# The normed output of the state space heads transposed by DMA in 16-bit halves instead of on TensorE

## Chip, cores and metric

The kernel runs on one core of a Trainium2 chip. The metric is the time of one execution in device microseconds (us), as the median of some runs. The engines are called PE (TensorE, the matmuls), ACT (ScalarE), DVE (VectorE), POOL (GpSimd) and SP (SyncE, which here issues nearly all DMA transfers). Each runs its own row of instructions in order.

## What is computed

One layer of a decoder: 256 tokens, width 2048. The input projection feeds a state space part (4 groups) and an attention part; both meet in one output projection; a feed-forward layer and a per-layer embedding follow. What the change touches is the end of each state space group: y times SiLU(z), normed over the group's 512 columns, times the gain, into the output projection.

```python
proj = a_in @ w_in[i]                     # [z | x,B,C | dt | q | k | v]
xbc  = silu(causal_dwconv(xbc, conv_w, conv_b))
y = ssd(xs_h, dt, a_neg, B, C) + d_skip * xs_h
y = y.reshape(b, s, SSM_INNER) * silu(z)
y_ssm = rmsnorm(y.reshape(b, s, 4, 512), ssm_norm_g.reshape(4, 512))
h = h + concat([y_ssm, y_att]) @ w_out
```

## The kernel before

The 256 tokens are two blocks of 128 (b = 0 and 1). A product in float32 is made of three in the faster fp32r type: both factors are split into a high and a low part, and high x high (L219), high x low (L220) and low x high (L221) are summed in PSUM. In the first chunk, that of B and C, the three are L317 to L319.

Weights come in tiles "w" of 128 x 2 x 512 numbers (512 KB). SP loads each (L207) into a ring of eight buffers (WR, L31); ACT casts it to the high part wh (L192) and DVE subtracts for the low part wl (L193), each in a ring of four buffers (WB). One tile feeds 12 matmuls of 512 columns: two k, two blocks, three products. A chunk of the input projection is eight such tiles into one pair of accumulators (acc0, acc1, one for each block); two such pairs are in PSUM. PSUM also holds two tiles "tr" for transposes on PE and two small ones "ms".

The left factors must stand with the contracted dimension on the partitions, so activations are transposed. transpose_split (L245) does that on PE (L252, 128 x 128 each) and splits the result from PSUM: ACT writes the high part with the gain (L195), DVE the low part (L196). For one group of y that is 8 transposes and four splits.

The stages: the chunk of B and C with the loads of x and, at its end, the small matmuls for dt (L337, L338), a copy of their result (L341) and the evacuation L352; then for each group g of the state space part ssd_x (a chunk for x, L352, the convolution with transposes L279, evacuation L266 and L268 into the single buffer "xc", the scan up to L503), ssd_gate (a chunk for z, evacuated with SiLU by L511) and ssd_end (L515). ssd_end multiplies y by z (L518), takes the squares on ACT (L519), the root on POOL (L187), scales y (L522) and transposes and splits it into yh and yl. Group 0 is projected right behind the z chunk of group 1 (project, L373); groups 1 to 3 wait in a list and are projected during attention.

Attention begins with a chunk of queries (q0), one for k and one for v. norm_rope (L605) evacuates a block of q0 into "qkr", which has a single buffer (L607), squares it (L609), sums (DVE, L611), takes the root (L185, POOL L187), scales (DVE L613, POOL L614) and rotates it on POOL (L621 to L623); L633 transposes the result on PE. The feed-forward part already moves data with the method that the change brings to y: POOL takes the halves of 32-bit numbers apart (L775), SP issues a transposing DMA on 16-bit numbers (L777), POOL puts the halves together (L778).

The order of each engine's instructions is set when the kernel is built, by a scheduler with a modelled timeline and by the buffers of each pool; the code gives only dependencies and a first order. A change of a few instructions so moves others too.

Of the kernel before, what the change touches and what calls it, by code (L numbers as in the profile page):

```python
# [14 lines left out]
U16 = mybir.dt.uint16  # L15
# [5 lines left out]
P = 128  # L21
T = 256
# [5 lines left out]
KG = 4  # L28
KW = 2
WB = 4  # L30
WR = 8  # L31
LINE = 512

HD = 64
# [31 lines left out]
def hybrid_layer(  # L66
# [20 lines left out]
    nc = tc.nc  # L87
    V, S, G, PE = nc.vector, nc.scalar, nc.gpsimd, nc.tensor
# [13 lines left out]
    def nm(s):  # L102
        uid[0] += 1
        return f"{s}_{uid[0]}"
# [3 lines left out]
    def sb(pool, shape, tag, dt=F32, bufs=None):  # L108
        kw = {} if bufs is None else {"bufs": bufs}
        size = math.prod(shape[1:]) * (2 if dt in (mybir.dt.bfloat16, U16) else 4)  # L110
        tags = sizes.setdefault(pool.id, {})
        tags[tag] = max(tags.get(tag, 0), -(-size // 32) * 32 * (bufs or pool.bufs))
        return pool.tile(shape, dt, tag=tag, name=nm(tag), **kw)
# [10 lines left out]
    def tr_tile():  # L124
        return ps_tr.tile([P, NC], F32, tag="tr", name=nm("tr"))
# [14 lines left out]
    def load_first(k, pieces=1):  # L140

        xt = sb(xin, [P, T], "xt", bufs=6)
        nc.sync.dma_start(xt, xT[:, k, :])
        w = sb(wp, [P, KW, NC], "w", bufs=WR)
        n = KW // pieces
# [34 lines left out]
    g_attn, g_ffn, g_ple, g_ssm = (gn[:, i * KT : (i + 1) * KT] for i in range(4))  # L180
    posi = sb(const, [P, NB], "posi", I32)

    def rstd(ss, n, cols, tag):
        t = sb(small, [P, cols], "rs_t")
        V.tensor_scalar(t, ss, 1.0 / n, EPS, op0=ALU.mult, op1=ALU.add)  # L185
        r = sb(small, [P, cols], tag)
        G.tensor_tensor(out=r, in0=t, in1=nhalf[:, :cols], op=ALU.pow)  # L187
        return r

    def split(src, hi, lo, scale=None):  # L190
        if scale is None:
            S.copy(hi, src)  # L192
            V.tensor_tensor(out=lo, in0=src, in1=hi.bitcast(F32), op=ALU.subtract)  # L193
        else:
            S.activation(out=hi, in_=src, func=AF.Copy, scale=scale)  # L195
            V.scalar_tensor_tensor(out=lo, in0=src, scalar=scale, in1=hi.bitcast(F32), op0=ALU.mult, op1=ALU.subtract)  # L196

    def load_w(src, kt=KW, pieces=1):

        w = sb(wp, [P, KW, NC], "w", bufs=WR)  # L200
        wh = sb(wp, [P, KW, NC], "wh", F32R)
# [43 lines left out]
    def transpose_split(src, lhs, k0, gain=None):  # L245

        for half in range(2):
            tr = tr_tile().rearrange("p (a t) -> p a t", a=2)
            for i in range(2):
                f = half * 2 + i  # L250
                for b in range(NB):
                    PE.transpose(tr[:, i, b * P : (b + 1) * P], src[b][:, f * P : (f + 1) * P], ident)  # L252
            k = k0 + half * 2
            if gain is None:
                h, l = lhs.t[k // KG]
                j = k % KG
                split(tr, h[:, j : j + 2, :], l[:, j : j + 2, :])
            else:
                for i in range(2):
                    h, l = lhs.part(k + i)  # L260
                    split(tr[:, i, :], h, l, gain[:, k + i : k + i + 1])
# [36 lines left out]
    with xin_:  # L298
        wd = sb(xin, [P, KT, 32], "wd")
        dhl = sb(xin, [P, KT, 64], "dhl", F32R)  # L300
        for k in range(KT):
# [24 lines left out]
            if k in (5, 9):  # L326
                b = k // 4 - 1
# [20 lines left out]
    def evac_scaled(acc, pool, tag, bufs=None):  # L348
        res = []
        for b in range(NB):  # L350
            t = sb(pool, [P, NC], f"{tag}{b}", bufs=bufs)
            S.activation(out=t, in_=acc[b], func=AF.Copy, scale=rx[:, b : b + 1])  # L352
            res.append(t)
        return res
# [29 lines left out]
    with tc.tile_pool(name="ssd", bufs=1) as sp, tc.tile_pool(name="dram", bufs=1, space=bass.MemoryType.DRAM) as dp:  # L384
        BT = sb(sp, [P, 4, T], "BT")
        CT = sb(sp, [P, 4, T], "CT")
        for c, (acc, dst) in enumerate(((acc_b, BT), (acc_c, CT))):
            t = evac_scaled(acc, sp, "ct", 1)
# [117 lines left out]
        def ssd_gate(g):  # L506
            acc = in_chunk(3 + 2 * g)
            zs = []
            for b in range(NB):
                z = sb(sp, [P, NC], f"z{b}")  # L510
                S.activation(out=z, in_=acc[b], func=AF.Silu, scale=rx[:, b : b + 1])  # L511
                zs.append(z)
            return zs

        def ssd_end(g, y, zs):  # L515
            ssy = sb(sp, [P, NB], "ssy", bufs=2)
            for b in range(NB):
                V.tensor_tensor(out=y[b], in0=y[b], in1=zs[b], op=ALU.mult)  # L518
                S.activation(out=zs[b], in_=y[b], func=AF.Square, accum_out=ssy[:, b : b + 1])  # L519
            ry = rstd(ssy, NC, NB, "ry")  # L520
            for b in range(NB):
                V.tensor_scalar_mul(y[b], y[b], ry[:, b : b + 1])  # L522
            yT = Lhs(yp_, KG, "y")
            transpose_split(y, yT, 0, g_ssm[:, 4 * g : 4 * g + 4])
            return (yT, w_out, g, 1)

        y = ssd_x(0)
        zs = ssd_gate(0)

        with tc.tile_pool(name="rope", bufs=1) as rp:  # L530
# [3 lines left out]
            for j in range(HALF):  # L534
                f = float(np.float32(THETA) ** np.float32(-2.0 * j / ROPE))
# [51 lines left out]
        for g in range(4):  # L587
            held.append(ssd_end(g, y, zs))
            if g < 3:
                y = ssd_x(g + 1)  # L590
                zs = ssd_gate(g + 1)
            if g < 1:
                project(*held.pop(0))
# [5 lines left out]
    with tc.tile_pool(name="att_s", bufs=2) as as_, tc.tile_pool(name="att", bufs=2, reuse_waits="tile") as ap_, tc.tile_pool(name="ps_sc", bufs=1, space=PSUM) as ps_sc:  # L599
# [108 lines left out]
        for b in range(NB):  # L708
            n = norm_rope(acc, b, kg_, "k")
# [185 lines left out]
```

## Time and profile before

| | |
|---|---|
| median of 3 runs | 1459.9 us (1458.42 to 1459.93) |
| profiled execution | 1461.06 us, its span 1459.3 us |
| mean granted clock of PE | 0.999 of full speed |
| PE busy | 1449.4 us (99%), 6660 matmuls |
| DVE, ACT, POOL busy | 988.1 us (68%), 792.5 us (54%), 238.1 us (16%, 208 instructions) |
| chain that ended last | PE 95%, DVE 2% |

The span is the time from the first to the last instruction in the profile; the profiled execution has 1.8 us more around it. A timeline row gives the start, the duration, the engine, the source line, the operation, the tile written "<-" the tiles read, the shape and the count of instructions merged into the row, and in brackets the idle time ahead of it and what ended that. Matmuls are pipelined: the time from one start to the next is what one costs, not its duration. "SPq" is SP's own queue.

### The profile page before, as it was taken

The page shows a single profiled execution, that of the slowest core. Times are in us where ns is not written, and L with a number is a line of the kernel's source. Part 1 is how long each engine was busy: PE and PEld are TensorE (multiplying, and loading weights), DVE is VectorE, ACT ScalarE, POOL GpSimd, SP SyncE. Part 2 cuts the span into 40 slices and gives each one's busy share as a digit, 9 for nine tenths or more (in the row PEclk, how much of TensorE's full clock was granted, in tenths as well). Part 3 has the DMA queues.
Part 4 walks back from the last instruction along what each step waited for, and adds up shares of the span by engine and source line. Part 5 has one row for each costly group of instructions (what it writes and reads, how often), then busy time and mean ns, then how long its engine had stood idle before and what let it go on. Part 6 is the DMA issues. An engine that isn't in the chain of part 4 may idle for free.

```text
span 1459.3 us, 18328 instructions
## 1 busy us (share of the span) xinstructions
PE 1449.4 (99%) x6660; PEld 1178.8 (81%) x6660; DVE 988.1 (68%) x1272; ACT 792.5 (54%) x1103; POOL 238.1 (16%) x208
## 2 busy tenths in 40 slices
PE   9999999999999999999999999999999999999998
PEld 7787888888777777788888888888888888888887
DVE  6678876765859678665766756774675577476854
ACT  6575555645646455466565545544554564455653
POOL 0002010016033020003333201311320231020000
PEclk9999999999999999999999999999999999999999
DMA  9665656546554545568778668767886877776671
GB/s 330 227 192 201 199 179 187 159 159 171 162 167 148 162 135 168 158 185 219 212 209 232 210 192 225 215 202 205 209 220 193 213 209 217 201 212 188 212 222 56
DMA packets 125900, 283.19 MB, mean 194 GB/s; under 512 B 55473, under 2 KB 58353, under 8 KB 125425
## 3 DMA queue, kind: packets, MB, share of 16 engines
q1 hardware_dynamic: 125376, 281.55, 66.2%
q8 instruction: 52, 0.85, 0.2%
q10 hardware_dynamic: 432, 0.48, 0.1%
q14 instruction: 40, 0.32, 0.1%
HBM read 268.32 MB, written 2.13 MB: 185 GB/s over the span
## 4 chain that ended last, share of the span: by engine, by line
PE 95%; DVE 2%; POOL 1%; DMA 1%; ACT 1%; issue 0%; SPq 0%; DVEq 0%; POOLq 0%
PE acc L220 29%; PE acc L219 29%; PE acc L221 29%; PE acc L317 1%; PE acc L319 1%; PE acc L318 1%; PE sc L647 1%; PE ms L495 1%; PE tr L683 1%; PE tr L674 1%; PE tr L252 1%; DVE wl L193 1%; DMA seg<-scr 0%; POOL rs L187 0%; ACT wh L192 0%
## 5 line engine op out<-in xcount | busy, mean ns | idle before, releaser
L193 DVE TENSOR_TENSOR wl<-w,wh 128x1024 fp32r<-128x1024 f32 (+1 forms) x493 | 629.1, 1279 | 383.7 <-ACT wh L192 375.4
L192 ACT CAST wh<-w 128x1024 fp32r<-128x1024 f32 (+1 forms) x493 | 516.2, 1048 | 517.9 <-PE acc L221 452.1
L220 PE MATMUL acc<-wl,ah 128*128 128x512 f32 x1280 | 500.9, 391 | 1.4 <-DVE wl L193 1.4
L221 PE MATMUL acc<-wh,al 128*128 128x512 f32 x1280 | 499.5, 391 | 0.0
L219 PE MATMUL acc<-wh,ah 128*128 128x512 f32 x1280 | 498.6, 392 | 0.0
L220 PEld LDWEIGHTS acc<-wl,ah 128*128 128x128 f32 x1280 | 240.4, 188 | 53.1 <-issue 2.1
L219 PEld LDWEIGHTS acc<-wh,ah 128*128 128x128 f32 x1280 | 240.4, 188 | 51.5 <-issue 2.0
L221 PEld LDWEIGHTS acc<-wh,al 128*128 128x128 f32 x1280 | 240.4, 188 | 49.6 <-issue 0.5
L220 PE MATMUL acc<-wl,gh 128*128 128x512 f32 x352 | 137.0, 389 | 0.0
L221 PE MATMUL acc<-wh,gl 128*128 128x512 f32 x352 | 137.0, 389 | 0.0
L219 PE MATMUL acc<-wh,gh 128*128 128x512 f32 x352 | 136.4, 389 | 0.0
L775 POOL COPY half<-u 128x1024 uint16<-128x1024 uint16 x44 | 62.1, 1425 | 261.3 <-ACT u L773 261.2
L220 PE MATMUL acc<-wl,yh 128*128 128x512 f32 x256 | 101.5, 397 | 0.0
L219 PE MATMUL acc<-wh,yh 128*128 128x512 f32 x256 | 101.0, 396 | 0.0
L221 PE MATMUL acc<-wh,yl 128*128 128x512 f32 x256 | 100.8, 395 | 0.0
L778 POOL COPY uc<-flip 128x1024 uint16<-128x1024 uint16 x44 | 55.9, 1271 | 172.5 <-DMA flip<-half 172.5
L359 DVE TENSOR_TENSOR h<-h,acc 128x512 f32<-128x512 f32 x112 | 73.8, 679 | 5.8 <-PE acc L221 5.8
L220 PEld LDWEIGHTS acc<-wl,gh 128*128 128x128 f32 x352 | 66.1, 188 | 13.7
L219 PEld LDWEIGHTS acc<-wh,gh 128*128 128x128 f32 x352 | 66.1, 188 | 13.7
L221 PEld LDWEIGHTS acc<-wh,gl 128*128 128x128 f32 x352 | 66.1, 188 | 13.6
L268 DVE SCALAR_TENSOR_TENSOR cv<-uc,fcw,cv 128x254 f32<-128x254 f32 (+1 forms) x176 | 73.8, 479 | 0.0
L220 PEld LDWEIGHTS acc<-wl,yh 128*128 128x128 f32 x256 | 48.1, 188 | 12.2 <-issue 2.9
(229 smaller groups left out, 1123.6 us busy)
## 6 DMA issues: line engine op xcount, KB each, us to landing
w<-in_w_up_dram SPq DMA_DIRECT2D x176, 512.0 KB, 4.2
w<-in_w_in_dram SPq DMA_DIRECT2D x126, 512.0 KB, 3.9
w<-in_w_down_dram SPq DMA_DIRECT2D x88, 512.0 KB, 4.3
w<-in_w_out_dram SPq DMA_DIRECT2D x64, 512.0 KB, 3.7
w<-in_w_pg_dram SPq DMA_DIRECT2D x32, 512.0 KB, 4.2
seg<-scr SPq DMA_DIRECT2D x8, 512.0 KB, 5.2
xt<-in_xT_dram SPq DMA_DIRECT2D x16, 128.0 KB, 7.0
h<-in_x_dram SPq DMA_DIRECT2D x2, 1024.0 KB, 8.6
```

What stands on the lines that cost most here:

```text
L192: S.copy(hi, src)
L193: V.tensor_tensor(out=lo, in0=src, in1=hi.bitcast(F32), op=ALU.subtract)
L219: PE.matmul(acc[b], lhsT=hi, rhs=wh[:, i, :], start=(k == 0), stop=False)
L220: PE.matmul(acc[b], lhsT=hi, rhs=wl[:, i, :], start=False, stop=False)
L221: PE.matmul(acc[b], lhsT=lo, rhs=wh[:, i, :], start=False, stop=(k == total - 1))
L252: PE.transpose(tr[:, i, b * P : (b + 1) * P], src[b][:, f * P : (f + 1) * P], ident)
L268: V.scalar_tensor_tensor(out=dst[:, s:], in0=ps[:, : T - s], scalar=taps[n - 1 - s], in1=dst[:, s:], op0=ALU.mult, op1=ALU.add)
L317: PE.matmul(acc[b], lhsT=h, rhs=wh[:, c, :], start=(k == 0), stop=False)
L318: PE.matmul(acc[b], lhsT=h, rhs=wl[:, c, :], start=False, stop=False)
L359: V.tensor_tensor(out=hs, in0=hs, in1=acc[b], op=ALU.add)
L775: G.tensor_copy(half.rearrange("p (a n) -> p a n", a=2), u_.bitcast(U16).rearrange("p (n a) -> p a n", a=2))
L778: G.tensor_copy(uc[:, :, b * P : (b + 1) * P].bitcast(U16).rearrange("p f (t a) -> p f t a", a=2), flip.rearrange("p (a f) t -> p f t a", ...
```

## The change

In ssd_end the eight transposes of a group on PE go. For each block POOL copies the scaled y into two planes of 16-bit halves, in the buffer of z that is no longer needed; SP issues one transposing DMA into a tile "flip" of 16-bit numbers (two buffers); POOL copies the transposed halves together into a tile "yt" of 32-bit numbers. yt takes the single buffer "xc" of the convolution. The split into yh and yl then reads yt, four times 128 x 256. To make room the ring of w tiles has seven buffers instead of eight. For all four groups together that is 32 transposes on PE fewer, 16 copies on POOL and 8 transposing DMAs more. Lines behind the change have numbers higher by ten: L607 is L617, L633 is L643.

```diff
--- before.py
+++ after.py
@@ -28,7 +28,7 @@
 KG = 4
 KW = 2
 WB = 4
-WR = 8
+WR = 7
 LINE = 512
 
 HD = 64
@@ -518,10 +518,20 @@
                 V.tensor_tensor(out=y[b], in0=y[b], in1=zs[b], op=ALU.mult)
                 S.activation(out=zs[b], in_=y[b], func=AF.Square, accum_out=ssy[:, b : b + 1])
             ry = rstd(ssy, NC, NB, "ry")
+            yt = sb(sp, [P, 4, T], "xc")
             for b in range(NB):
                 V.tensor_scalar_mul(y[b], y[b], ry[:, b : b + 1])
+                half = zs[b].bitcast(U16).rearrange("p (a n) -> p a n", a=2)
+                G.tensor_copy(half, y[b].bitcast(U16).rearrange("p (n a) -> p a n", a=2))
+                flip = sb(sp, [P, 8, P], "flip", U16, 2)
+                nc.sync.dma_start_transpose(flip, half.rearrange("p a n -> p (a n)"))
+                G.tensor_copy(
+                    yt[:, :, b * P : (b + 1) * P].bitcast(U16).rearrange("p f (t a) -> p f t a", a=2),
+                    flip.rearrange("p (a f) t -> p f t a", a=2),
+                )
             yT = Lhs(yp_, KG, "y")
-            transpose_split(y, yT, 0, g_ssm[:, 4 * g : 4 * g + 4])
+            for f in range(4):
+                split(yt[:, f, :], *yT.part(f), g_ssm[:, 4 * g + f : 4 * g + f + 1])
             return (yT, w_out, g, 1)
 
         y = ssd_x(0)
```

The new order differs between the end of the B/C chunk and the first part of attention. In the names below the numbers count buffers. The first place is ACT around the SiLU evacuation of z of group 1 (L511), behind which project(0) starts. Before:

```order
L195 ACTIVATE yh0_215_1135<-tr_217_1137,gains_3_91 128x256
L195 ACTIVATE yh0_215_1135<-tr_218_1146,gains_3_91 128x256
L195 ACTIVATE yh0_215_1135<-tr_217_1137,gains_3_91 128x256
L195 ACTIVATE yh0_215_1135<-tr_218_1146,gains_3_91 128x256
L192 CAST wh_300_1561<-w_299_1560 128x1024
L192 CAST wh_303_1579<-w_302_1578 128x1024
L467 COPY Bt_224_1179<-tr_223_1177 128x128
L266 ACTIVATE xc_253_1331<-tr_254_1332,scw_15_133 128x256
L192 CAST wh_308_1601<-w_307_1600 128x1024
L511 ACT_TABLE_LOAD
L511 ACTIVATE z0_295_1554<-acc0_269_1408,rx_27_145 128x512
L511 ACTIVATE z1_296_1556<-acc1_270_1409,rx_27_145 128x512
```

and now:

```order
L192 CAST wh_294_1536<-w_293_1535 128x1024
L192 CAST wh_301_1560<-w_300_1559 128x1024
L192 CAST wh_304_1578<-w_303_1577 128x1024
L192 CAST wh_309_1600<-w_308_1599 128x1024
L511 ACT_TABLE_LOAD
L511 ACTIVATE z0_296_1553<-acc0_270_1407,rx_27_145 128x512
L511 ACTIVATE z1_297_1555<-acc1_271_1408,rx_27_145 128x512
L195 ACTIVATE yh0_218_1144<-xc_215_1133,gains_3_91 128x256 x4
L192 CAST wh_312_1618<-w_311_1617 128x1024
```

The four yh of group 0 stood nine instructions ahead of the table load and now stand right behind the second SiLU; they read xc, the tile yt, as one row "x4".

The second place is ACT at the entry to attention, with the evacuations of q0 (L607 before, L617 now) and the four yh of group 3; acc0_517, acc1_518 before and acc0_521, acc1_522 now are q0's accumulators. Before:

```order
L195 ACTIVATE yh0_502_2597<-tr_504_2599,gains_3_91 128x256
L195 ACTIVATE yh0_502_2597<-tr_505_2608,gains_3_91 128x256
L607 ACTIVATE qkr_543_2788<-acc0_517_2642,rx_27_145 128x512
L609 ACTIVATE qkn_544_2790<-qkr_543_2788 128x512
L195 ACTIVATE yh0_502_2597<-tr_504_2599,gains_3_91 128x256
L195 ACTIVATE yh0_502_2597<-tr_505_2608,gains_3_91 128x256
L192 CAST wh_583_2939<-w_582_2938 128x1024
L192 CAST wh_586_2957<-w_585_2956 128x1024
L607 ACTIVATE qkr_554_2817<-acc1_518_2643,rx_27_145 128x512
L192 CAST wh_589_2975<-w_588_2974 128x1024
L609 ACTIVATE qkn_555_2819<-qkr_554_2817 128x512
```

and now, where the casts to wh_623, wh_626, wh_629 and wh_632 are those of the first four tiles of the v chunk:

```order
L192 CAST wh_623_3064<-w_622_3063 128x1024
L192 CAST wh_626_3082<-w_625_3081 128x1024
L192 CAST wh_629_3100<-w_628_3099 128x1024
L195 ACTIVATE yh0_508_2603<-xc_505_2592,gains_3_91 128x256 x4
L192 CAST wh_632_3118<-w_631_3117 128x1024
L617 ACTIVATE qkr_547_2784<-acc0_521_2638,rx_27_145 128x512
L619 ACTIVATE qkn_548_2786<-qkr_547_2784 128x512
L617 ACTIVATE qkr_558_2813<-acc1_522_2639,rx_27_145 128x512
L619 ACTIVATE qkn_559_2815<-qkr_558_2813 128x512
L192 CAST wh_635_3136<-w_634_3135 128x1024
L192 CAST wh_638_3154<-w_637_3153 128x1024
L192 CAST wh_641_3172<-w_640_3171 128x1024
```

The two evacuations of q0 now stand next to each other, behind the cast of the fourth tile of v, and the later casts stand behind both.

The third place is PE where the v chunk starts (acc0_616, acc1_617 before, 620 and 621 now). Before:

```order
L220 MATMUL acc1_566_2847<-wl_590_2976,ah3_24_142 128x512
L221 MATMUL acc1_566_2847<-wh_589_2975,al3_25_143 128x512
L219 MATMUL acc0_616_3065<-wh_619_3068,ah0_18_136 128x512
L220 MATMUL acc0_616_3065<-wl_620_3069,ah0_18_136 128x512
L221 MATMUL acc0_616_3065<-wh_619_3068,al0_19_137 128x512
L219 MATMUL acc1_617_3066<-wh_619_3068,ah0_18_136 128x512
L220 MATMUL acc1_617_3066<-wl_620_3069,ah0_18_136 128x512
L221 MATMUL acc1_617_3066<-wh_619_3068,al0_19_137 128x512
L219 MATMUL acc0_616_3065<-wh_619_3068,ah0_18_136 128x512
```

and now, from the last matmul of the k chunk:

```order
L221 MATMUL acc1_570_2843<-wh_593_2971,al3_25_143 128x512
L219 MATMUL acc0_620_3061<-wh_623_3064,ah0_18_136 128x512
L220 MATMUL acc0_620_3061<-wl_624_3065,ah0_18_136 128x512
L221 MATMUL acc0_620_3061<-wh_623_3064,al0_19_137 128x512
L219 MATMUL acc0_620_3061<-wh_623_3064,ah0_18_136 128x512
L220 MATMUL acc0_620_3061<-wl_624_3065,ah0_18_136 128x512
L221 MATMUL acc0_620_3061<-wh_623_3064,al0_19_137 128x512
L219 MATMUL acc0_620_3061<-wh_626_3082,ah0_18_136 128x512
L220 MATMUL acc0_620_3061<-wl_627_3083,ah0_18_136 128x512
```

The next 16 matmuls write acc0_620 too, from the second, third and fourth tile, so that the first 24 of the chunk go to acc0; only then does acc1_621 come. Before, the two accumulators took turns from the start.

## Rows read from the trace of the kernel before

**Rows 1.** The page of the profile: busy time, share and count of PE, the subtraction on DVE (busy, mean ns of one, idle before), and the shares of the chain that ended last by engine.

```profile
PE 1449.4 (99%) x6660; PEld 1178.8 (81%) x6660; DVE 988.1 (68%) x1272; ACT 792.5 (54%) x1103; POOL 238.1 (16%) x208
...
PE 95%; DVE 2%; POOL 1%; DMA 1%; ACT 1%; issue 0%; SPq 0%; DVEq 0%; POOLq 0%
...
L193 DVE TENSOR_TENSOR wl<-w,wh 128x1024 fp32r<-128x1024 f32 (+1 forms) x493 | 629.1, 1279 | 383.7 <-ACT wh L192 375.4
```

**Rows 2.** The list of PE's waits over the whole span: what waited for what, us in total, times, longest.

```profile
PE acc L220 <- DVE wl L193: 1.4, 1, 1.4
PE tr L279 <- ACT ct L352: 1.2, 1, 1.2
```

**Rows 3.** PE's timeline around the eight transposes of y of group 0.

```profile
149.18 0.40 PE L221 MATMUL acc<-wh,al 128*128 128x512 f32 x1
149.42 1.04 PE L252 MATMUL tr<-ident,yc 128*128 128x128 f32 x8
150.21 0.48 PE L219 MATMUL acc<-wh,ah 128*128 128x512 f32 x1
150.53 0.39 PE L220 MATMUL acc<-wl,ah 128*128 128x512 f32 x1
150.76 0.40 PE L221 MATMUL acc<-wh,al 128*128 128x512 f32 x1
```

**Rows 4.** ACT's timeline at the end of the B/C chunk.

```profile
56.31 1.05 ACT L192 CAST wh<-w 128x1024 fp32r<-128x1024 f32 x1 [1.67 <-PE acc L319]
57.26 0.36 ACT L341 COPY hsq<-ms 64x256 f32<-64x256 f32 x1
57.52 1.25 ACT L352 ACTIVATE ct<-acc,rx 128x512 f32<-128x512 f32 x2
```

**Rows 5.** PE's timeline at the same place.

```profile
55.88 0.39 PE L319 MATMUL acc<-wh,al 128*128 128x512 f32 x1
56.11 0.28 PE L338 MATMUL ms<-ah,dhl 128*64 128x256 f32 x1
...
56.81 0.28 PE L338 MATMUL ms<-ah,dhl 128*64 128x256 f32 x1
58.31 0.41 PE L279 MATMUL tr<-ident,ct 128*128 128x128 f32 x2 [1.21 <-ACT ct L352]
```

**Rows 6.** PE's timeline at the transposition of the second block of q0.

```profile
341.13 0.39 PE L219 MATMUL acc<-wh,ah 128*128 128x512 f32 x1
341.94 0.66 PE L633 MATMUL tr<-ident,qkn 128*128 128x128 f32 x4 [0.42 <-POOL qkn L623]
```

**Rows 7.** ACT's timeline at the SiLU evacuation of z of group 1.

```profile
159.18 1.28 ACT L511 ACT_TABLE_LOAD   x1
160.47 1.27 ACT L511 ACTIVATE z<-acc,rx 128x512 f32<-128x512 f32 x2
161.63 1.05 ACT L192 CAST wh<-w 128x1024 fp32r<-128x1024 f32 x1
```

**Rows 8.** PE's timeline from the last matmul of that z chunk to the first of project(0).

```profile
160.22 0.39 PE L221 MATMUL acc<-wh,al 128*128 128x512 f32 x1
160.44 0.39 PE L219 MATMUL acc<-wh,yh 128*128 128x512 f32 x1
```

**Rows 9.** The tile "flip" of the feed-forward part: duration in ns (minimum, median, maximum), first and last start, and the time from a DMA's issue to its landing.

```profile
L777 SPq DMA_TRANSPOSE flip<-half x44: 1231/1233/2119, 662.4 to 1293.0; - x44
L778 POOL COPY uc<-flip x44: 1157/1162/2235, 667.0 to 1298.8; 128x1024 uint16<-128x1024 uint16 x44
...
DMA to landing us min/median/max: 3.9/5.6/7.1
```

**Rows 10.** The copy ahead of it, in the same form.

```profile
L775 POOL COPY half<-u x44: 1035/1041/2209, 658.5 to 1288.5; 128x1024 uint16<-128x1024 uint16 x44
```

**Rows 11.** ACT's timeline at the evacuation of q0 (L607 for block 0 and block 1).

```profile
318.22 1.05 ACT L192 CAST wh<-w 128x1024 fp32r<-128x1024 f32 x1 [1.67 <-PE acc L221]
319.17 0.83 ACT L195 ACTIVATE yh<-tr,gains 128x256 fp32r<-128x256 f32 x2
319.90 0.69 ACT L607 ACTIVATE qkr<-acc,rx 128x512 f32<-128x512 f32 x1
...
328.71 0.69 ACT L607 ACTIVATE qkr<-acc,rx 128x512 f32<-128x512 f32 x1 [3.13 <-POOL qkn L614]
```

**Rows 12.** ACT's timeline at a later evacuation of queries, again block 0 and block 1.

```profile
417.64 0.69 ACT L607 ACTIVATE qkr<-acc,rx 128x512 f32<-128x512 f32 x1 [0.39 <-PE acc L221]
...
423.84 0.69 ACT L607 ACTIVATE qkr<-acc,rx 128x512 f32<-128x512 f32 x1 [1.12 <-POOL qkn L614]
```

**Rows 13.** PE's timeline at its longest idle gap.

```profile
124.22 0.61 PE L219 MATMUL acc<-wh,ah 128*128 128x512 f32 x2
126.23 0.50 PE L220 MATMUL acc<-wl,ah 128*128 128x512 f32 x1 [1.40 <-DVE wl L193]
126.57 0.39 PE L221 MATMUL acc<-wh,al 128*128 128x512 f32 x1
```

**Rows 14.** PE's timeline at the start of the kernel.

```profile
11.16 1.88 PE L317 MATMUL acc<-wh,ah 128*128 128x512 f32 x4
12.86 0.41 PE L318 MATMUL acc<-wl,ah 128*128 128x512 f32 x1
13.11 0.39 PE L319 MATMUL acc<-wh,al 128*128 128x512 f32 x1
```

## Prediction, made before the changed kernel was run

> **What bounds the kernel now.** I read the page first, then the list of PE's waits, then single stretches of the timeline where the change touches something. The page [rows 1] shows PE busy 99% of the span and 95% of the chain that ended last, so any microsecond taken off PE's own work counts, and so does any microsecond for which PE has to wait. Other engines count only where PE comes to wait for them. The list of waits [rows 2] has 1.4 and 1.2 us as its longest: between PE's instructions there is next to nothing to win, and much room for a new wait to lose. The pace is that of a 512-column matmul, one each 0.23 us from start to start [rows 3], so a weight tile of 12 matmuls lasts 2.75 us and a chunk of eight tiles 22.0 us. PE, ACT, DVE, POOL and SP each run their own row of instructions in order; the question for every moved instruction is whether PE stands behind it.
>
> **What the change removes.** Each group's eight transposes of y run from 149.42 to 150.21, and the second matmul after them starts 0.32 after the first, not 0.23 [rows 3]: 0.79 + 0.09 = 0.88 us of PE, four times 3.52 us. No other engine hides that; all of it lies on the path. **-3.52.**
>
> Two effects of the new order go with it. At the end of the b/c chunk PE waits 1.21 us for ACT's evacuation [rows 5], which stands behind a cast that waits for the last L319 and behind L341, the copy of ms [rows 4]. In the new order ten, not seven, of the small L337/L338 matmuls stand behind that last L319. They start 0.115 us apart (56.11 to 56.81, six steps), so the cast can start 0.35 us earlier; but L341 still needs the last of them, which ends at 57.09, and L341 started at 57.26 already. The gain lies between 0.1 and 0.35, nearer the former since L341 is what is late next: **-0.15.** And the rotated queries of block 1 were transposed (L633) 0.81 us after the matmul before, where 0.23 is the pace [rows 6]; in the new order this transposition stands far behind its rotation: **-0.58.**
>
> **What it adds beside other work.** Sixteen POOL copies and eight transposing DMAs. The same three steps run 44 times in the FFN: the halves taken apart 1.04 us, the DMA 5.6 us to landing (7.1 at most), the halves put together 1.16 us (2.24 at most) [rows 9, 10]. POOL is busy for 16% of the span, so 16 copies, some 18 us, cost nothing as long as nobody waits for the 8 us that one chain takes. The split reads SBUF instead of PSUM: two PSUM tiles are left to the conv transposes. The ring of seven w tiles instead of eight covers 7 x 2.75 = 19 us against loads that land within some 4 to 5 us; SP loses 1.23 us per transposing DMA [rows 9]. I cost this at nothing; if a load were late it would show as a wait of ACT's cast for a w. The next group's conv must wait for the split's last read of the shared "xc" buffer; its first row in the order stands behind that split anyway, and the result is wanted a chunk later.
>
> **Where PE will wait (1): project(0).** In the order before, ACT makes the four yh well ahead of the Silu of z(1). In the new order they stand directly behind it (the first pair of order excerpts), and project(0)'s first matmul on PE stands directly behind z(1)'s last: PE, which passed here with no gap, 160.22 to 160.44 [rows 8], now waits for z0, z1 and the first yh. By ACT's times of before the table load ends and z0 starts at 160.47, the next instruction after z1 at 161.63 [rows 7]; a yh from SBUF takes about 0.5 us (two on tr take 0.83 together [rows 11]), so PE goes on at 162.15: 1.7 us lost. If ACT comes earlier, z1 is bound by PE alone: last matmul ends at 160.61, z1 lasts 0.69 and hands over after 0.59, yh 0.5, 0.06 to hand on: PE goes on at 161.8: 1.4 us. I take the middle: **+1.55.** The flips do not decide here: the second is issued at about 152, lands by 157.6 and is put together by 158.8, at worst 161.3 by the longest rows.
>
> **Where PE will wait (2): the entry to attention.** In the order before, ACT evacuated q0's first block (L607) among the casts of the k chunk, with nothing waiting for it [rows 11]. In the new order the four yh of group 3 stand between the third and fourth cast of the v chunk, and both evacuations of q0 (now L617) behind them (second pair of excerpts). The v chunk uses q0's accumulators, so PE stops at its first matmul until L617 has read acc0. The cast ahead of L617 needs the buffer of the k chunk's last tile, that is, PE at the end of k: 0.2 us later it starts (56.11 to 56.31, [rows 4, 5]), L617 follows 0.95 later (318.22 to 319.17, [rows 11]), lasts 0.69, and 0.1 goes for the handover: 1.95 us at least. Are the flips later than that? Counted from the start of the k chunk, SP issues the second flip of group 3 behind a load that needs the slot of k's last tile: four tiles of PE 11.0, wait and cast 1.25, the DVE subtraction 1.28 [rows 1], the load's issue 0.3: 13.8. Landing 5.6 and copy 1.16 make 20.6; the cast before the yh ends at about 20.5; four yh at 0.36 end at 22.0, and the fourth cast could not start before 22.2 anyway. So by the medians the flips cost nothing, by the longest rows (7.1 and 2.24) they end at 23.1 and the stall is 4.3. I take 2.4, near the medians. **+2.4.**
>
> Then PE has 24 matmuls of acc0 in a row (the third pair), 5.5 us, and needs acc1: L617 of block 1. It has one buffer "qkr", free when POOL's product of block 0 has read it: 6.2 us from one evacuation to the next where nothing is in the way (417.64 to 423.84 [rows 12]), 8.8 at this very place before (319.90 to 328.71 [rows 11]). I take 6.2, since ACT now waits in L617 with all later casts behind it and DVE therefore has no subtraction to run against POOL. PE begins 0.8 after L617 began, is through at 6.3, and may go on at 6.2 + 0.69 + 0.1 = 7.0: **+0.7**, or 3.3 by the longer row.
>
> **The sum.** -3.52 - 0.15 - 0.58 + 1.55 + 2.4 + 0.7 = **+0.4 us.** The profiled run took 1461.06 us, of which 1459.3 is the span; it would become 1461.5. The three timed runs have their median 1.2 us below it, 1459.9; I give the forecast on their footing: **1460.3 us**, no change that can be measured.
>
> **A rule of the Trainium skill that speaks against the change.** "VectorE: DVE Perf Modes", section "Rules for kernel authors", says to transpose 128x128 on TensorE if a PSUM destination will do, and by DMA otherwise. PSUM did do here. Its table of paths (section "The three transpose paths") counts 390 ns for one on TensorE; this trace has 0.11 us for one of eight in the pipeline [rows 3], and the trace decides. By the page's figure the estimate of the removed work would be 32 x 0.39 = 12.5 us, and the sum -8.6.
>
> **Rivals.** (A) The gain stands: no new wait, because ACT reaches the yh and q0 in time. Then -3.52 - 0.15 - 0.58 = -4.25, 1455.6 us. For it: PE's list of waits has hardly a row [rows 2], so the order has kept such things hidden before. Against it: in both places PE's next matmul reads what ACT has still to write. Chance 0.10, with the cases where one of the waits is missing and the other short.
>
> (B) Slower: the chain of q0's block 0 takes the 8.8 us of [rows 11], not 6.2. DVE's subtraction and POOL's power and product then run at the same time as before. The second stall is 3.3 instead of 0.7: 1462.9; with a flip that lands at 7.1 and a copy of 2.24 ahead of it the first is 4.3 instead of 2.4: 1464.8. It decides as soon as the second evacuation begins more than 8.7 us after the first. Chance 0.16.
>
> (C) The clock: at the start, before PE had run without gaps, 512-column matmuls stood 0.43 us apart until 12.86, then 0.25 [rows 14], the lower and the upper of the two levels, 1.2 and 2.4 GHz. After an idle gap of 1.40 at 124 to 126 us the next two stood 0.34 apart, the first of them 0.50 long, and the granted clock stayed up [rows 13]. The new gaps, 1.55 and 2.4, are little longer; if one of them brought the lower level for some 15 matmuls, it would cost 15 x 0.2 = 3 us: 1463.3. Chance 0.04. The Trainium skill, "TensorE: Matmul & The Clock Gate", section "Part 1: The HAM clock gate", says that the engine falls back to half its clock when it has been idle; by that rule (C) would follow, and the trace, where 1.4 us idle did not do it, agrees only that short gaps do no harm.
>
> **How the numbers follow.** About 0.2% (2.9 us) is what a measurement of this kernel can tell from no change: faster is under 1457.0, slower over 1462.8. The forecast has 0.70. Its ends: the first wait 1.4 to 1.7, the second 1.95 to 4.3 with most of it under 3, the third 0 to 2: 1459 to 1462.6; 1457.4 if one is cut short by an early ACT. Faster 0.10 is (A); slower 0.20 is (B) and (C). The range of 1457.4 to 1463.6 leaves out most of (A) and the double case of (B).
>
> **What the profile after would show.** No L252 with yc; POOL 224 instructions instead of 208, the new copies near 1.0 to 1.2 us; flips landing in 4 to 7 us. In PE's list of waits, acc waiting for yh of L195 near 160 us (about 1.5) and acc waiting for qkr of L617 near 335 to 343 us (about 2.4, then 0.7); the one for POOL's qkn gone. If the first two are absent, (A) is right; if the third is over 2.5, (B); matmuls 0.43 apart behind a gap would be (C). I would be wrong altogether if casts wait for w tiles, or if DVE's subtractions become slower wherever POOL copies run.

## The result and the profile after

The changed kernel takes 1461.49 us (median of 17 runs, 1460.27 to 1465.96), the kernel before in the same series 1459.43 us (median of 17). By the two medians it is 2.1 us slower. The ratio, which goes by all runs and not by the medians, is 1.0020 with a 95% interval of 1.0014 to 1.0027, that is 2.9 us (2.0 to 3.9). No change (1.0000) lies outside the interval, though the size is only about the 0.2% which the prediction took as the least that can be told. The profiled execution has a span of 1462.0 us, 2.7 more than that of before.

The page of the changed kernel answers to the first row of [rows 1]:

```profile
PE 1446.7 (99%) x6628; PEld 1176.0 (80%) x6628; DVE 988.8 (68%) x1272; ACT 793.2 (54%) x1103; POOL 264.8 (18%) x224
```

The 32 transposes are gone from PE (6660 to 6628), the 16 copies are on POOL (208 to 224). PE is 2.7 us less busy and the span 2.7 us longer, so PE stands idle longer than before. The list of PE's waits, to be held against [rows 2]: what waited for what, us in total, times, longest.

```profile
PE acc L219 <- ACT qkr L617: 2.3, 1, 2.3
PE acc L219 <- ACT yh L195: 2.2, 1, 2.2
...
PE tr L279 <- ACT ct L352: 1.1, 1, 1.1
PE tr L725 <- DVE s L721: 0.9, 1, 0.9
...
PE acc L220 <- DVE wl L193: 0.8, 1, 0.8
```

The first two rows are new and are the two places of the prediction: yh at project(0), qkr at the entry to attention. The fourth is new and was not foreseen: transposes of the second block of k. The wait for the rotated queries [rows 6] is gone, those at the B/C chunk and for wl are 0.1 and 0.6 shorter.

**Project(0).** PE's timeline, to be held against [rows 8]:

```profile
157.78 0.39 PE L221 MATMUL acc<-wh,al 128*128 128x512 f32 x1
160.41 0.50 PE L219 MATMUL acc<-wh,yh 128*128 128x512 f32 x1 [2.23 <-ACT yh L195]
160.75 0.39 PE L220 MATMUL acc<-wl,yh 128*128 128x512 f32 x1
...
161.54 0.63 PE L219 MATMUL acc<-wh,yh 128*128 128x512 f32 x1
161.96 0.63 PE L220 MATMUL acc<-wl,yh 128*128 128x512 f32 x1
```

From the last matmul of z(1) to the first of project(0) it takes 2.63 us instead of 0.22. And soon behind the gap the steps are 0.42 (161.54 to 161.96), not 0.23. ACT's timeline in the same stretch, against [rows 7]:

```profile
156.88 1.28 ACT L511 ACT_TABLE_LOAD   x1 [0.34 <-PE acc L221]
158.18 1.27 ACT L511 ACTIVATE z<-acc,rx 128x512 f32<-128x512 f32 x2
159.85 1.71 ACT L195 ACTIVATE yh<-xc,gains 128x256 fp32r<-128x256 f32 x4 [0.40 <-POOL xc L528]
```

The two z end at 159.45, and the yh begin 0.40 later, when POOL has put the second flip together. That copy, in POOL's timeline, and ahead of it the issue of its DMA in that of SP's queue:

```profile
152.79 1.24 SPq L527 DMA_TRANSPOSE flip<-z  x1
```

```profile
158.66 1.15 POOL L528 COPY xc<-flip 128x1024 uint16<-128x1024 uint16 x1 [2.56 <-DMA flip<-z]
```

**The entry to attention.** ACT's timeline, against [rows 11]:

```profile
333.82 1.05 ACT L192 CAST wh<-w 128x1024 fp32r<-128x1024 f32 x1 [1.67 <-PE acc L221]
335.55 1.71 ACT L195 ACTIVATE yh<-xc,gains 128x256 fp32r<-128x256 f32 x4 [0.68 <-POOL xc L528]
337.17 1.03 ACT L192 CAST wh<-w 128x1024 fp32r<-128x1024 f32 x1
338.10 0.68 ACT L617 ACTIVATE qkr<-acc,rx 128x512 f32<-128x512 f32 x1
...
344.33 0.69 ACT L617 ACTIVATE qkr<-acc,rx 128x512 f32<-128x512 f32 x1 [4.89 <-POOL qkn L624]
```

The chain is the one of the prediction, but with the flip 0.68 late, so that the yh and not PE's last matmul of k hold up the fourth cast (337.17). The second evacuation comes 6.2 us behind the first (338.10 to 344.33), as in [rows 12].

**The clock.** Windows of PE around both gaps: busy time of PE, PEld, DVE, ACT and POOL with counts, then the granted clock, the DMA share and GB/s.

```profile
157.20:160.40 3.20, 0.97 (x5) 0.47 (x3) 0.61 (x2) 2.79 (x5) 1.15 (x1) 1.00 1.06 366
160.40:164.90 4.50, 4.49 (x13) 3.54 (x14) 4.05 (x9) 3.00 (x6) 0.00 (x0) 0.62 0.39 148
165.00:170.00 5.00, 5.00 (x24) 4.12 (x23) 2.66 (x5) 1.97 (x3) 0.00 (x0) 1.00 0.25 89
338.80:342.40 3.60, 3.56 (x9) 2.86 (x10) 1.81 (x4) 0.63 (x1) 1.64 (x1) 0.53 0.59 199
```

The granted clock is 1.00 up to the gap, 0.62 in the 4.5 us behind the first and 0.53 in the 3.6 us behind the second: the lower level for most of these stretches, then 1.00 again. What it costs: 4.5 x 0.38 = 1.7 us and 3.6 x 0.47 = 1.7 us.

**The start.** The two profiles also differ where nothing was changed. Before, four L317 in a row began at 11.16 and took 1.88 us [rows 14]; the same four now:

```profile
9.57 1.20 PE L317 MATMUL acc<-wh,ah 128*128 128x512 f32 x4 [0.67 <-ACT wh L192]
```

PE came to the upper level earlier and stands 1.6 us ahead. That is an accident of this execution: in the second profile of the same program (experiment 5) the four begin at 10.54, behind steps of 0.43. So the difference of the two spans understates what the change costs in it.

**The sum of the two profiles.** Transposes -3.5; B/C -0.1; the wait for wl -0.6; L633 -0.6; project(0) 2.63 - 0.23 = +2.4, its slow steps +1.7; entry +2.5 (336.12 to 338.83 in PE's row, less 0.23), its slow steps +1.7; k's transposes +0.9; start -1.6. Together +2.8 of the measured 2.7; small moves elsewhere are left out.

The profiled execution took 1463.71 us, 2.2 more than the median. Where the clock stays up, PE waits another 0.6 at the second evacuation (experiment 5); without the slow steps and the start, the terms give -3.5 - 0.1 - 0.6 - 0.6 + 2.4 + 2.5 + 0.6 + 0.9 = +1.6. That is near the 2.1 of the medians, so most of the difference needs no slow steps. The 17 times fit this: nine lie from 1460.3 to 1461.5, six from 1462.1 to 1463.7 and two at 1465.9, where those of the kernel before lie from 1458.4 to 1461.4. That the upper ones are executions with slow steps is likely from the profiles, but not shown for each.

### The profile page after: what moved, and what is told of

It reads as the page before. It is cut to its first block, busy times and chain, and to the rows that moved or that the text cites. A ratio compares the mean times of both kernels' runs of the same rounds, so it can differ in the third digit from the quotient of the medians.

```text
span 1462.0 us, 18295 instructions
## 1 busy us (share of the span) xinstructions
PE 1446.7 (99%) x6628; PEld 1176.0 (80%) x6628; DVE 988.8 (68%) x1272; ACT 793.2 (54%) x1103; POOL 264.8 (18%) x224
## 4 chain that ended last, share of the span: by engine, by line
PE 92%; DVE 2%; DMA 2%; issue 1%; ACT 1%; POOL 1%; SPq 0%; DVEq 0%; POOLq 0%; ACTq 0%
PE acc L220 28%; PE acc L219 28%; PE acc L221 28%; PE tr L693 1%; PE sc L657 1%; DMA w<-in_w_in_dram 1%; PE ms L495 1%; DMA seg<-scr 1%; DVE wl L193 1%; PE tr L684 1%; PE acc L318 1%; PE acc L319 1%; PE acc L317 1%; PE tr L252 0%; ACT wh L192 0%
## 5 line engine op out<-in xcount | busy, mean ns | idle before, releaser
L788 POOL COPY uc<-flip 128x1024 uint16<-128x1024 uint16 x44 | 60.6, 1377 | 166.7 <-DMA flip<-half 166.6
L219 PEld LDWEIGHTS acc<-wh,yh 128*128 128x128 f32 x256 | 48.5, 189 | 13.3 <-ACT yh L195 2.7
```

What stands on the lines that cost most here:

```text
L219: PE.matmul(acc[b], lhsT=hi, rhs=wh[:, i, :], start=(k == 0), stop=False)
L788: G.tensor_copy(uc[:, :, b * P : (b + 1) * P].bitcast(U16).rearrange("p f (t a) -> p f t a", a=2), flip.rearrange("p (a f) t -> p f t a", ...
```

## Experiments

Ratios are to the kernel before, measured on the same chip in the same series, with 95% intervals; they go by all runs and so differ a little from the ratio of the two medians.

| kernel | median us | before | ratio (interval) |
|---|---|---|---|
| ring of 7, y on PE | 1459.24 | 1459.56 | 0.9988 (0.9967 to 1.0010) |
| only group 0 by DMA | 1462.47 | 1459.56 | 1.0026 (1.0016 to 1.0036) |
| groups 1 to 3 | 1462.32 | 1459.56 | 1.0021 (1.0012 to 1.0030) |
| groups 1 and 2 | 1458.22 | 1459.56 | 0.9992 (0.9984 to 1.0001) |
| the change again | 1462.11 | 1459.19 | 1.0021 (1.0012 to 1.0030) |
| the change, first gap filled | 1461.88 | 1459.19 | 1.0019 (1.0010 to 1.0027) |
| own pool, project(0) later | 1457.78 | 1459.19 | 0.9992 (0.9983 to 1.0001) |
| groups 0 to 2, project(0) later | 1457.50 | 1459.19 | 0.9985 (0.9977 to 0.9994) |
| own pool | 1462.14 | 1459.69 | 1.0015 (1.0007 to 1.0024) |
| project(0) later | 1460.95 | 1459.69 | 1.0009 (1.0000 to 1.0018) |
| groups 0 to 2, project(0) later, two qkr | 1455.09 | 1459.69 | 0.9970 (0.9959 to 0.9982) |
| all four, own pool, project(0) later, two qkr | 1460.39 | 1459.69 | 1.0004 (0.9995 to 1.0013) |

### 1. The shorter ring alone

```diff
-WR = 8
+WR = 7
```

> The kernel before with seven w buffers instead of eight, y still transposed on PE. Theory (the time of the changed kernel is made of two waits of PE, at project(0) and at the entry to attention): no difference to the kernel before, within 1 us, and no cast waits for a w. Rival (the shorter ring costs time by itself): about 2 us slower, with waits of casts for w in the profile.

No difference can be seen, and no cast waits for a w behind the first chunk. The rival's 2 us lie outside the interval. The ring is not where the time went.

### 2 to 4. Some groups only

```diff
+            if g in (0,):          # (1, 2, 3) and (1, 2) in the other two
                 yt = sb(sp, [P, 4, T], "xc")
...
+            else:
+                transpose_split(y, yT, 0, g_ssm[:, 4 * g : 4 * g + 4])
```

> Only group 0 is transposed by DMA, groups 1 to 3 on PE as before; seven w buffers. Theory: the 0.9 us of its transposes are gone, PE waits at project(0) for yh as in the changed kernel (2.2 us), and if the clock falls behind that gap, another 1.7 us: 1.5 to 3.2 us slower than before, and no wait for qkr at the entry to attention. Rival (each group's copies and transposing DMAs cost about the same, spread over the run): a quarter of the change's 2 us, 0.5 us slower, without one long wait.

> Groups 1 to 3 by DMA, group 0 on PE as before. Theory: -2.6 us of transposes, no wait for yh at project(0), the wait for qkr at the entry to attention as in the changed kernel (2.3 us) and up to 1.7 us of low clock behind it: between 0.5 faster and 2 slower than before. Rival (cost spread evenly over groups): 1.5 us slower with no long wait.

> Groups 1 and 2 by DMA, groups 0 and 3 on PE as before. Theory: both places keep their old order, neither wait appears, and 1.8 us of transposes are saved: 1.5 to 2 us faster than before. Rival (cost spread evenly over groups): 1 us slower.

One group of four, the first, costs 2.9 us by itself; the two in the middle are 1.3 faster, a little short of what was expected and with an interval that just touches no change. Groups 1 to 3 missed their expectation: 2.8 slower, not 2 at most. So the cost is not spread over groups; it comes with the first and the last. It can't be added up from the parts, though: 2.9 and 2.8 make 5.7, and all four together cost 2.1, since each kernel has its own order and so its own waits. The waits of PE, first with group 0 alone:

```profile
PE tr L731 <- DVE s L727: 2.2, 1, 2.2
PE acc L219 <- ACT yh L195: 1.9, 1, 1.9
```

with groups 1 to 3:

```profile
PE acc L219 <- ACT qkr L623: 3.7, 1, 3.7
```

and with groups 1 and 2:

```profile
PE tr L731 <- DVE s L727: 1.6, 1, 1.6
```

(L623, L727 and L731 are L617, L721 and L725 of the changed kernel.) yh is waited for with group 0 and qkr with group 3, each where expected. The wait for the transposes of k's second block also stands in kernels whose entry to attention is untouched: that was in no theory, and it is part of what group 0 alone costs and of what groups 1 and 2 do not save. With group 0 alone the terms are +2.0 at project(0), +2.2 for k, -0.9 for the transposes and -0.6 for L633, together +2.7: the larger half lies at k. Why k's block comes late there stays open; experiment 11 shows only what removes it.

### 5. The changed kernel once more

> The changed kernel once more. Theory (two waits of 2.2 to 2.4 us and, in some executions, 1.7 us of low clock behind each): 1 to 4 us slower than before, the waits for yh and for qkr again in the list; the steps of 0.43 us behind them may come behind one wait and not behind the other. Rival (the clock behind the gaps falls every time): both stretches of 0.43 us again.

The first gap again has slow steps behind it, the second has not. PE's timeline at both:

```profile
161.74 0.79 PE L219 MATMUL acc<-wh,yh 128*128 128x512 f32 x1 [2.63 <-ACT yh L195]
162.33 0.63 PE L220 MATMUL acc<-wl,yh 128*128 128x512 f32 x1
162.75 0.63 PE L219 MATMUL acc<-wh,yh 128*128 128x512 f32 x1
...
339.89 0.50 PE L219 MATMUL acc<-wh,ah 128*128 128x512 f32 x1 [2.21 <-ACT qkr L617]
340.24 0.40 PE L220 MATMUL acc<-wl,ah 128*128 128x512 f32 x1
340.48 0.40 PE L221 MATMUL acc<-wh,al 128*128 128x512 f32 x1
...
346.14 0.50 PE L219 MATMUL acc<-wh,ah 128*128 128x512 f32 x1 [0.47 <-ACT qkr L617]
```

Here the steps behind the second gap are 0.24, and so PE is through its 24 matmuls of acc0 before the second evacuation is done and waits once more, 0.86 us from start to start (345.28 to 346.14 in PE's row): the third wait of the prediction, which the slow clock had covered in the first profile. The clock behind the gap so differs between two executions of one program, so the rival, the same slow steps every time, is out.

### 6. The first gap filled

```diff
+                for _ in range(busy):          # 10, ahead of project(0)'s first product
+                    PE.matmul(acc[0], lhsT=aT(0, 0)[0], rhs=w[0][:, 0, :], start=True, stop=True)
```

> The changed kernel with ten matmuls more on PE between the last of z(1) and the first of project(0): they write project(0)'s accumulator ahead of its start and are overwritten, and they lie within the 2.6 us in which PE waited for yh. Theory: the wait's end is ACT's and does not move, the idle time shrinks to some 0.3 us, and behind it the steps are 0.23 us in every profile: up to 1.7 us faster than the changed kernel. Rival (the slow steps come from operands that have just been written, or the added matmuls delay the work): still 0.43 behind, the same time or up to 2.3 us more.

PE's timeline (L229 is the added line):

```profile
157.09 0.39 PE L221 MATMUL acc<-wh,al 128*128 128x512 f32 x1
157.31 2.43 PE L229 MATMUL acc<-wh,ah 128*128 128x512 f32 x10
159.59 0.39 PE L219 MATMUL acc<-wh,yh 128*128 128x512 f32 x1
159.81 0.39 PE L220 MATMUL acc<-wl,yh 128*128 128x512 f32 x1
160.04 0.40 PE L219 MATMUL acc<-wh,yh 128*128 128x512 f32 x1
```

The first product with yh starts 2.5 us behind the last of z(1), about as late as before, and the steps behind it are 0.22 from the first on. Operands just written do not slow PE: it reads a yh just written at 0.22 to 0.23 a step here, and also with group 0 alone, behind a gap of 1.87. That the filling kept the clock up is likely but not shown by one profile, since the clock stayed up behind some unfilled gaps too. The median, 0.2 us below the changed kernel's in the same series, doesn't show the 1.7: the clock does not fall behind every gap, and the gap at the entry to attention is still there. So the price of the clock is shown in profiles, not in medians.

### 7 and 8. Two ways around both waits

```diff
-WR = 7
+WR = 6
...
+    yx = mix.enter_context(tc.tile_pool(name="yx", bufs=1))
...
-            yt = sb(sp, [P, 4, T], "xc")
+            yt = sb(yx, [P, 4, T], "yt")
...
-                flip = sb(sp, [P, 8, P], "flip", U16, 2)
+                flip = sb(yx, [P, 8, P], "flip", U16, 2)
...
                 y = ssd_x(g + 1)
+                if g == 1:
+                    project(*held.pop(0))
                 zs = ssd_gate(g + 1)
-            if g < 1:
-                project(*held.pop(0))
```

The second kernel has only the last part of this, with seven w buffers, and keeps group 3 on PE (experiments 2 to 4 show how).

> The changed kernel with yt and flip in a pool of their own, which outlives that of the state space part, so that the buffers of attention come free as soon as the last transposing DMA has read, and with project(0) behind the x chunk of group 2 instead of directly behind the z chunk of group 1; six w buffers for room. Theory: neither wait appears, 3.5 us of transposes stay saved: 2.5 to 4 us faster than before. Rival (the costs lie in the copies, the DMAs or the shorter ring): about as slow as the changed kernel.

> Groups 0 to 2 by DMA, group 3 on PE, project(0) behind the x chunk of group 2; seven w buffers. Theory: neither wait appears and 2.6 us of transposes are saved: 2 to 3 us faster than before, less what the transposes of k's second block wait. Rival (cost with each group transposed by DMA): 1 to 2 us slower.

Both are on the fast side of before, by 1.4 and 1.7 us; for the first the interval just touches no change, and its expectation of 2.5 to 4 was missed. The second, expected 2 to 3 faster less the wait of k's block (1.6 in its list), did a little better than that. Neither has a wait for yh or qkr in its list. Its longest row in the first, and in the second:

```profile
PE tr L644 <- POOL qkn L634: 1.8, 2, 1.6
```

```profile
PE tr L731 <- DVE s L727: 1.6, 1, 1.6
```

With the two long waits gone, the next chain in line shows: the norm and rotation of q and k on POOL.

### 9 and 10. Each way alone

The diffs are the two parts of the one above, the first with six w buffers.

> The changed kernel with yt and flip in a pool of their own that outlives the state space part's; six w buffers for room; project(0) where it was. Theory (q0's evacuation waited for the memory that yt and flip held): the wait for qkr at the entry to attention is gone, the wait for yh at project(0) of 2.2 to 2.6 us stays: 1 to 2.5 us faster than the changed kernel, within 1 us of the kernel before. Rival (the evacuation stands late for another reason): the wait for qkr stays, no faster than the changed kernel.

> The changed kernel with project(0) behind the x chunk of group 2 and nothing else; seven w buffers. Theory: the wait for yh at project(0) is gone, the one for qkr of 2.2 us and more stays: 2 to 3 us faster than the changed kernel, within 1 us of the kernel before. Rival (the wait only moves to the next place that needs yh): a wait for yh elsewhere, same time as the changed kernel.

With the own pool, ACT's timeline at the entry to attention (L618 is L617 of the changed kernel, L196 is L195):

```profile
317.77 0.68 ACT L618 ACTIVATE qkr<-acc,rx 128x512 f32<-128x512 f32 x1
...
321.02 1.71 ACT L196 ACTIVATE yh<-yt,gains 128x256 fp32r<-128x256 f32 x4 [0.43 <-POOL yt L529]
```

The evacuation stands ahead of the yh, twenty microseconds earlier than the 338.10 of the changed kernel, and nothing waits for it: what held it was the memory of yt and flip, which attention's buffers take over (the ring went to six w buffers with it, which was not varied alone). But the time was not won: 1462.14 is 2.4 us slower than before, where at most 1 was expected. The list of waits:

```profile
PE tr L644 <- POOL qkn L634: 1.9, 2, 1.6
PE acc L220 <- ACT yh L196: 1.4, 1, 1.4
...
PE tr L478 <- ACT xc L473: 0.9, 1, 0.9
```

The wait for yh became shorter because PE meets another one ahead of it (xc, 0.9), and the rotated queries are waited for instead of qkr. The theory was right on the cause and wrong on the worth.

With project(0) later alone the wait for yh is gone and appears nowhere else, but the one at the entry grew:

```profile
PE acc L219 <- ACT qkr L617: 3.8, 1, 3.8
```

The stretch of slow steps behind it was longer too (13 matmuls at 0.43 or near it). The kernel is 1.3 us slower than before, a little over the microsecond that was expected at most, and gains less on the changed kernel than the expected 2 to 3 (ratio 1.0009, there 1.0020).

### 11 and 12. A second buffer for qkr

```diff
-            r = sb(ap_, [P, NC], "qkr", bufs=1)
+            r = sb(ap_, [P, NC], "qkr", bufs=2)
```

added to the kernels of 8 and of 7.

> Groups 0 to 2 by DMA, group 3 on PE, project(0) behind the x chunk of group 2, seven w buffers, and qkr with two buffers instead of one. Theory (with one qkr buffer the second block of k is normed a chain later, and its transposes make PE wait 1.6 us): that wait shrinks, 1 to 1.6 us faster than the same without the second buffer, 3 to 4 us faster than before. Rival (POOL's chain sets the time, not the buffer): the wait stays, no difference.

> All four groups by DMA, yt and flip in a pool of their own, project(0) behind the x chunk of group 2, qkr with two buffers, six w buffers. Theory: neither of the two long waits, 3.5 us of transposes saved, and the wait for rotated queries (1.8 us with one qkr buffer) shorter or later: 2 to 4 us faster than before. Rival (six w buffers or PE waiting for the rotation eat it): within 1 us of the kernel before, with waits for qkn or for w in the list.

The first is the fastest kernel of the study: 4.6 us below before, ratio 0.9970. Its whole list of waits, from the longest:

```profile
PE acc L317 <- ACT wh L192: 1.5, 2, 1.0
PE tr L279 <- ACT ct L352: 1.1, 1, 1.1
PE ms L155 <- PEq L901: 0.8, 1, 0.8
PE acc L220 <- DVE wl L193: 0.8, 1, 0.8
```

Behind the first 125 us there is no wait left, the one for k's second block included. It gained more than that wait's 1.6. Neither the second qkr buffer nor the later project(0) was tried on the kernel before with y on PE, so how much of the 4.6 us is owed to the transposing DMAs stays open. The other kernel missed its expectation: 0.7 us slower than before, not 2 to 4 faster. Its longest wait:

```profile
PE tr L644 <- POOL qkn L634: 3.1, 2, 2.8
```

and PE's timeline there:

```profile
333.24 0.66 PE L644 MATMUL tr<-ident,qkn 128*128 128x128 f32 x4 [2.84 <-POOL qkn L634]
...
333.96 0.39 PE L221 MATMUL acc<-wl,ah 128*128 128x512 f32 x1
334.19 0.39 PE L222 MATMUL acc<-wh,al 128*128 128x512 f32 x1
```

With two buffers the product of block 1 stands on POOL between the rotations of block 0, and PE's transposes of block 0 are in its row already. So with all four groups by DMA the entry to attention remains the weak place, whichever way it was arranged here.

## Why the prediction was right, and where its terms were not

The forecast was 1460.3 us and no measurable change; 1461.5 came out, in the range, and the direction that it gave for the sum, a little slower, was the one measured. But the slowdown can be told from no change, and the sum of +0.4 is 1.7 us short of the 2.1 between the medians. By its steps:

- **Removed transposes, -3.52.** Right: 32 fewer on PE, and groups 1 and 2 alone, where nothing is given back at the two places, come out 1.3 us below before (the interval just touches no change); the sum of their terms is -1.8 for the transposes, -0.6 for L633 and +1.6 for k, -0.8.
- **B/C chunk -0.15, L633 -0.58.** 1.37 instead of 1.50 us from L338 to L279 (-0.13), and the wait for L633 gone: right. That the wait for wl at 124 us would be 0.6 shorter was not foreseen.
- **Copies, DMAs and the shorter ring at nothing.** Right: experiment 1, and experiments 2 to 4 show no cost for each group.
- **Project(0), +1.55.** Right in place and cause, too small: 2.4. The step "the flips do not decide here" failed: the yh began 0.40 behind the z. The second flip was to be put together 1.4 us ahead of PE's last matmul of z(1) (158.8 against 160.22) and came 2.0 behind it (159.81 against 157.78). About half of the 3.4 us between is that PE reaches this matmul 11.4 us after DVE begins to scale y, not 13.0 (146.39 now, 147.25 before, in DVE's rows); the other half is that the DMA is issued 6.4 us after that beginning, not 4.75, behind two w loads in SP's row. And the table load waited for PE (0.34), so z0 came 0.40 behind PE's last matmul, not 0.25.
- **Entry to attention, +2.4.** Right in place and size: 2.5. But "by the medians the flips cost nothing" failed here too: the yh waited 0.68 for the second flip, and the fourth cast, which by the prediction waits for PE at the end of k, could have started at 336.3 and started behind the yh at 337.17. Without the flip the wait would have been some 1.8 (an estimate from these rows); that 2.4 fits is in part luck, a value taken between two bounds. What made the order so was not in the prediction, which took it from the order alone: the memory of yt and flip (experiment 9).
- **Second evacuation of q0, +0.7.** The 6.2 us were right, those of [rows 12] and not the 8.8 of [rows 11]. The wait itself is 0.6 in one profile and absent in the other, where PE was slowed for 1.7 us and had no time to wait.
- **Rival (C), the clock, at 0.04.** Far too low as a chance that it happens. Its mechanism was there, behind one or both gaps, at 1.7 us each. I had counted 1.55 and 2.4 us of gap as "little longer" than the 1.40 of [rows 13]. The median came out in the range all the same, since the clock doesn't fall each time and the terms without it make +1.6; the profiled execution, 1463.71, lies just above the range.
- **Not in it at all:** the transposes of k's second block, 0.9.
- **A sign that came and meant nothing.** The prediction would be "wrong altogether" if DVE's subtractions became slower beside POOL's copies. They do: 2.06 us instead of 1.22 in the first of these rows, from the scaling of group 3, and the two copies take 3.14 together, where one by itself takes 1.04 [rows 10].

```profile
321.38 3.14 POOL L525 COPY z<-yc 128x1024 uint16<-128x1024 uint16 x2 [0.66 <-ACT wh L192]
321.56 2.06 DVE L193 TENSOR_TENSOR wl<-w,wh 128x1024 fp32r<-128x1024 f32 x1
```

But PE's only wait for wl is the 0.8 at 124 us, ahead of the first copy (147.01): the subtractions had the time to spare.

So the removed work and the two places were right, and that the sum fell in the range is partly luck: project(0) was 0.85 too small, k's 0.9 was missing, the flips were late at both places, and the clock, where it fell, came on top. Rival (A) is excluded by the list of waits, rival (B) by the 6.2 us.

**The rule of the Trainium skill** ("VectorE: DVE Perf Modes", "Rules for kernel authors") that prefers TensorE for a 128x128 transpose into PSUM came out right for groups 0 and 3 with the order as it was; for groups 1 and 2 the DMA was no worse and, by an interval that just touches no change, 1.3 us better. What decided was not the price of a transpose on either path, but whether someone stands waiting when the longer path ends: 13 us at project(0) and 15 at the entry, from the start of DVE's scaling (146.4 and 320.75) to the yh (159.85 and 335.55). "TensorE: Matmul & The Clock Gate" ("Part 1: The HAM clock gate") says that PE falls back to half its clock when idle; these traces show steps of 0.43 us, that level, behind some of the gaps and not behind others, and the trace agrees only that far.

## What to carry to other kernels

Taking work off the busiest engine pays only where the detour ends before somebody needs its result: look at what that engine does right behind the place, and move the consumer, not only the producer. A longer detour also keeps its buffers longer; ask whose memory they are and what is to be placed there next. And where PE has had no gap for a long time, price a new gap at its own length plus what the clock may take behind it, and give the second part as a range that begins at nothing.

## What was not expected of the hardware

Behind idle gaps on PE the granted clock fell in some cases and not in others. By the wait in the bracket of the row: 1.40 us (the kernel before), 1.9 (group 0 alone), 2.1 (the first gap filled, at the entry), 2.21 (the change again, at the entry), another 2.21 (group 0 alone, at k's second block) and 2.84 (experiment 12, at the rotated queries) left the steps at 0.23 to 0.24 from the second or third on; 2.23, 2.33 (the change), 2.63 (the change again), 3.7 (groups 1 to 3) and 3.8 (project(0) later) were followed by steps of 0.43 for 7 to 13 matmuls, some after a few quick ones. One program did both at the same place, and a gap of 2.84 left the clock up where one of 2.23 did not, so the length of the gap alone does not decide. No rule is drawn from so few.

That a lower clock can hide a wait was new as well: slowed behind the first gap at the entry, PE came 1.7 us later to the next accumulator and found it free, where in the other profile it waited.
